# Conformer and DeltaNet trunk step: where the memory values stand in the convolution, which engine sums, and two margins of the planner

## The chip, the core and the metric

The kernel runs on one of the eight cores of one Trainium2 chip. A core has five engines that run side by side and wait for each other by semaphores: TensorE (PE in the profile; PEld is its weight load), VectorE (DVE), ScalarE (ACT), GpSimd (POOL) and SyncE (SP), which issues most DMAs. SBUF is the on-chip working memory, PSUM the memory of eight banks into which TensorE writes its sums. The metric is the device time of one execution in microseconds, and the figure for a kernel is the median of its runs.

## The reference

One inference step of a two-layer encoder runs for two groups of tokens that share all weights: 256 prompt tokens of one new stream and 16 tokens of each of eight running streams, 384 tokens of 1024 features. Each layer is a feed-forward half-step, a token mixer, a cross-attention into 256 memory tokens and a second feed-forward half-step, each with a norm before and after. The mixer is a Conformer convolution in layer 0 and a gated DeltaNet in layer 1. The change is in and around the convolution:

```python
u = h @ w_in + b_in
val, gate = jnp.split(u, 2, axis=-1)
u = val * jax.nn.sigmoid(gate)
hist = jnp.concatenate([conv_buf.astype(u.dtype), u], axis=1)
c = causal_depthwise_conv(hist, dw) + dw_b          # 31 taps on each feature
c = jax.nn.silu(layer_norm(c, ln_g, ln_b))
return c @ w_out + b_out, hist[:, -(CONV_W - 1):]
```

The memory keys and values of the prompt, `mem_prompt @ xa_wk` and `mem_prompt @ xa_wv` of both layers, are outputs too. They depend on no token, so they can be computed anywhere ahead of the attention that reads them.

## The kernel before

**Three matmuls for one.** Weights lie in device memory as chunks of 128 x 1024 fp32 numbers. `get` (L295) loads a chunk into one of three `raw` buffers, ScalarE casts it to the shorter type fp32r (`whi`), and the rest, the low part `wlo`, is the difference of the two. It is taken by VectorE, or by GpSimd where the chunk is listed in `SLOW` (L92). Eight pairs `whi`, `wlo` are held at a time, taken in the order of the calls. Activations are split in the same way (`hTh`, `hTl`, and `rbh`, `rbl`), and each product is three fp32r matmuls. Sums, transposes and the memory keys go through TensorE in fp32 instead, where one matmul leaves two records in the profile.

**Emission and planner.** The program is first emitted as a list of operations for each engine, by generators that stand for tasks beside each other (`spawn`, `pump`, `until`). They keep rough clocks of their own, and the buffers and PSUM banks are handed out in this emission. Then `Scheduler` (L323) builds the dependence graph of all operations and orders every engine's queue: a list schedule by priority (`early`), whose priorities come from a schedule run backwards (`late`), in three passes, of which the shortest plan is kept (`order`). `LAT` (L327) has the planner's delay from the end of an operation on one engine to the start of a dependent one on another. What depends on nothing urgent fills gaps. Each engine carries out its queue strictly in that order.

**The convolution** (`conv`, L1060). Features lie on partitions, 128 of them in each of eight tiles (`KT`), tokens on the free axis. For each tile, two projections (`cg`, `cv`) of 24 fp32r matmuls of 384 columns each give gate and value; `glu` forms the gated input and its history. The task `taps` takes the tiles in pairs: VectorE multiplies and adds one tap after the other into two PSUM banks (the taps that read only the cache of running streams were done during the first feed-forward). When a pair is finished, TensorE adds its two tiles into the mean, with a matrix of 1/1024 (`onesd`, L1125), and a PSUM bank is held for that sum from the first pair on.

**Memory values** (`kv_split`, L942) are emitted behind the eight tiles. They load the memory tokens into `rbh` and `rbl`, and for each layer and head one unit of two chunks and 48 fp32r matmuls of 256 columns, eight units in all, each with a PSUM bank, a copy and a store. **Memory keys** (`kv`, L1006) are units of eight fp32 matmuls of 256 columns; `KV` says how many are emitted at each place: three at the end of the first feed-forward, five behind the convolution's tiles, two with its output projection.

**The layer norm** (`ln`, L1155) goes by three groups of 128 tokens. VectorE subtracts the mean, ScalarE squares, TensorE sums the squares of the eight feature tiles with eight matmuls against `onesd` (L1171), VectorE adds EPS, GpSimd takes the power of -1/2, TensorE spreads the result over the partitions with a matmul against the identity, VectorE multiplies, and ScalarE applies the silu. Then the output projection (`co`) follows group by group, with a norm chain (`chain`, L663) behind each group that leads to the attention's first matmuls.

Of the kernel before, what the change touches and what calls it, by code (L numbers as in the profile page):

```python
# [11 lines left out]
ALU = mybir.AluOpType  # L12
# [3 lines left out]
P = 128  # L16
# [21 lines left out]
FIRST_SLOW = 2  # L38
# [12 lines left out]
POOLTRUE = 1  # L51
LANES = 8
# [270 lines left out]
class Scheduler:  # L323
# [3 lines left out]
    LAT = {"P": {"P": 0, "A": 197, "V": 197}, "A": {"P": 275, "V": 131, "G": 159, "A": 131},  # L327
           "V": {"P": 260, "A": 128, "V": 127, "G": 155}, "G": {"P": 311, "A": 77, "V": 76, "G": 104}}
# [113 lines left out]
    def early(self, prio):  # L442
# [12 lines left out]
        for _ in ops:  # L455
            best, e, i = self.pick(free, now, later, lambda i: -prio[i])
            o = ops[i]
            cost = o.cost
            if o.nbytes:
                best = max(best, lanes[e][0])  # L460
            at[i] = best
            if o.table and o.table != table:
                table = o.table
                cost += 1283.0
            end = free[e] = best + cost
            if o.nbytes:
                dma = max(dma, end + DMA_IN) + o.nbytes / 360.0
                end = dma + DMA_OUT
                lanes[e] = lanes[e][1:] + [end]
            last = max(last, end)  # L470
            for j in o.succ:
                rd[j] = max(rd[j], end + (0.0 if o.nbytes else self.LAT[e].get(ops[j].eng, 150)))
                npred[j] -= 1
                if not npred[j]:
                    heapq.heappush(later[ops[j].eng], (rd[j], j))
# [66 lines left out]
class Model:  # L542
# [399 lines left out]
    def kv_split(self):  # L942
# [3 lines left out]
        vt = E.vt  # L946
# [14 lines left out]
        for l in range(2):  # L961
            for h in range(XH):

# [16 lines left out]
                E.store(self.O["pkv"][l, h][:, 512:1024], r)  # L980
        self.free(rh)
        E.vt = vt
# [77 lines left out]
    def conv(self, chains, post, pre):  # L1060
# [32 lines left out]
        def taps():  # L1093
            for c0 in range(0, KT, 2):
# [26 lines left out]
                if not means:  # L1121
                    means.append((yield from self.gbank()))
                for c in cs:
                    self.free(hist[c][1], hist[c][3])
                    E.mm(means[0][0][:, 0:NTOK], self.onesd, cO[:, c, :], c == 0, c == KT - 1)  # L1125
            self.conv_end = e

        means = []
# [3 lines left out]
        for c in range(KT):  # L1132
# [9 lines left out]
            if c + 2 < KT:  # L1142
                prefetch(c + 2)

        self.kv_split()
# [9 lines left out]
        def ln(t, dep):  # L1155
# [11 lines left out]
            e = E.act(qv, x, AF.Square, dep=e)  # L1167
            yield e
            o, b = yield from self.gbank()
            for k in range(KT):  # L1170
                e = E.mm(o[:, 0:P], qv[:, k, :], self.onesd, k == 0, k == KT - 1)  # L1171
# [752 lines left out]
```

## Time and profile before

| | |
|---|---|
| median of 3 runs | 1880.22 us (1877.89 to 1883.22) |
| profiled execution, device time | 1880.99 us |
| its span, first to last instruction | 1879.2 us |
| TensorE busy (matmul) | 1848.6 us, 98% |
| VectorE busy | 986.4 us, 52% |
| ScalarE busy | 765.5 us, 41% |
| GpSimd busy | 252.6 us, 13% |
| granted TensorE clock, mean | 0.998 of full speed |

Busy time counts the time in which at least one instruction of the engine is under way. Matmuls overlap in the pipeline, so the duration of one record is longer than what it adds to the engine's time; the step from one start to the next shows that. The convolution begins with its first projection at 321.4 us, its taps end at 457.7 us, and its output projection begins at 474.6 us. A row of a timeline joins instructions of the same kind that follow each other; `x28` is their number.

### The profile page before, as it was taken

To read this page: it belongs to the slowest core of one execution; us is meant where nothing else is said; L and a number is where in the kernel's file an instruction comes from. 1 tells how busy PE (TensorE), PEld (TensorE's weight loads), DVE (VectorE), ACT (ScalarE), POOL (GpSimd) and SP (SyncE) were. 2 spreads that over 40 slices of the span, in tenths; PEclk is the share of its full clock that TensorE was granted. 3 is DMA by queue.
4 is the path that set the end of the run, shared out by engine and by line. 5 is a ranking of instruction groups with operands and counts; after the bars stand their busy time and mean duration, and the time that the engine had idled before them with its cause. 6 is when DMAs were issued, how large, how long until landed. Compare 5 with 4: busy or idle time off the path is not lost.

```text
span 1879.2 us, 26770 instructions
## 1 busy us (share of the span) xinstructions
PE 1848.6 (98%) x10479; PEld 1658.3 (88%) x10479; DVE 986.4 (52%) x1681; ACT 765.5 (41%) x1443; POOL 252.6 (13%) x420
## 2 busy tenths in 40 slices
PE   8999999999999999999999999999999999999998
PEld 7988998998877799999899999899998777899997
DVE  5456335898542643333643333687877644533333
ACT  4332334334542532323533333676665544432332
POOL 1000003568100100000200000233231101000000
PEclk9999999999999999999999999999999999999999
DMA  8534435448487534444434344333334583534441
GB/s 303 163 119 128 135 113 148 128 141 258 165 302 275 153 113 129 128 124 134 155 114 128 120 131 124 107 102 104 103 118 154 193 328 108 157 124 124 135 123 45
DMA packets 88622, 279.81 MB, mean 149 GB/s; under 512 B 17904, under 2 KB 20464, under 8 KB 88496
## 3 DMA queue, kind: packets, MB, share of 16 engines
q1 hardware_dynamic: 86368, 272.47, 45.4%
q0 software_dynamic: 2128, 5.63, 0.9%
q8 instruction: 82, 1.34, 0.3%
q14 instruction: 44, 0.36, 0.1%
HBM read 266.14 MB, written 11.92 MB: 148 GB/s over the span
## 4 chain that ended last, share of the span: by engine, by line
PE 63%; ACT 2%; DVE 2%; DMA 1%; POOL 1%; issue 1%; DVEq 0%; POOLq 0%; ACTq 0%; SPq 0%
PE ps L253 60%; PE ps L265 2%; PE ps L285 2%; DMA raw<-in_w 1%; DVE wlo L203 1%; ACT big L196 1%; POOL stat L203 1%; DVE big L216 1%; ACT whi L195 1%; PE ps L278 0%; ACT L196 0%; ACT hTl L196 0%; DVE hTl L203 0%; ACT big L195 0%; POOL stat L210 0%
## 5 line engine op out<-in xcount | busy, mean ns | idle before, releaser
L203 DVE TENSOR_TENSOR wlo<-raw,whi 128x1024 fp32r<-128x1024 f32 x341 | 415.3, 1223 | 566.9 <-ACT whi L195 564.8
L195 ACT CAST whi<-raw 128x1024 fp32r<-128x1024 f32 x377 | 393.7, 1050 | 710.7 <-PE ps L253 615.3
L253 PE MATMUL ps<-hTh,whi 128*128 128x384 f32 (+1 forms) x1680 | 505.6, 341 | 1.7 <-ACT big L196 0.7
L253 PE MATMUL ps<-hTl,whi 128*128 128x384 f32 (+1 forms) x1680 | 501.7, 339 | 0.1
L253 PE MATMUL ps<-hTh,wlo 128*128 128x384 f32 x1680 | 500.1, 339 | 0.0
L253 PEld LDWEIGHTS ps<-hTh,whi 128*128 128x128 f32 x1680 | 309.7, 188 | 14.4 <-ACT big L196 6.1
L253 PEld LDWEIGHTS ps<-hTl,whi 128*128 128x128 f32 x1680 | 310.2, 188 | 10.3 <-issue 2.8
L253 PEld LDWEIGHTS ps<-hTh,wlo 128*128 128x128 f32 x1680 | 309.6, 188 | 5.9 <-issue 0.7
L253 PE MATMUL ps<-whi,rbh 128*128 128x512 f32 (+1 forms) x800 | 242.2, 379 | 2.4 <-DVE big L216 2.3
L253 PE MATMUL ps<-whi,rbl 128*128 128x512 f32 (+1 forms) x800 | 244.1, 378 | 0.0
L253 PE MATMUL ps<-wlo,rbh 128*128 128x512 f32 (+1 forms) x800 | 240.9, 377 | 0.6 <-POOL wlo L203 0.6
L253 PE MATMUL ps<-big 128*128 128x128 f32 (+3 forms) x1144 | 216.0, 316 | 9.4 <-DMA big<-in_w 6.8
L253 PEld LDWEIGHTS ps<-big 128*128 128x128 f32 x1144 | 178.6, 192 | 36.8 <-issue 13.0
L253 PEld LDWEIGHTS ps<-wlo,rbh 128*128 128x128 f32 x800 | 150.2, 189 | 26.6 <-issue 1.6
L253 PEld LDWEIGHTS ps<-whi,rbh 128*128 128x128 f32 x800 | 149.2, 189 | 26.0 <-ACT big L196 2.6
L253 PEld LDWEIGHTS ps<-whi,rbl 128*128 128x128 f32 x800 | 150.1, 189 | 22.4 <-issue 0.8
L210 POOL TENSOR_SCALAR stat<-stat 128x1 f32<-128x1 f32 (+2 forms) x48 | 17.6, 367 | 1023.1 <-ACT hTl L196 1004.5
L203 DVE TENSOR_TENSOR big<-big,ps 128x384 f32<-128x384 f32 (+4 forms) x131 | 67.4, 521 | 81.5 <-PE ps L253 64.3
L216 DVE SCALAR_TENSOR_TENSOR ps<-big,cols,ps 128x384 f32<-128x384 f32 (+12 forms) x232 | 107.4, 553 | 0.4
L203 POOL TENSOR_TENSOR wlo<-raw,whi 128x1024 fp32r<-128x1024 f32 x36 | 86.7, 2421 | 49.5 <-ACT whi L195 43.7
L253 PE MATMUL ps<-whi,hTh 128*128 128x512 f32 x240 | 86.6, 402 | 2.5 <-ACT hTh L195 2.1
L253 PE MATMUL ps<-whi,hTl 128*128 128x512 f32 x240 | 85.4, 400 | 0.0
(91 smaller groups left out, 1488.8 us busy)
## 6 DMA issues: line engine op xcount, KB each, us to landing
raw<-in_w SPq DMA_DIRECT2D x380, 512.0 KB, 4.0
big<-in_ck SPq DMA_DIRECT2D x32, 512.0 KB, 6.0
big<-in_cv SPq DMA_DIRECT2D x32, 512.0 KB, 6.0
big<-in_w SPq DMA_DIRECT2D x21, 512.0 KB, 6.4
big<-in_npre SPq DMA_DIRECT2D x8, 512.0 KB, 7.4
big<-in_npost SPq DMA_DIRECT2D x8, 512.0 KB, 6.5
big<-out_pkv SPq DMA_DIRECT2D x8, 512.0 KB, 5.8
big<-in_state SPq DMA_DIRECT2D x8, 512.0 KB, 4.4
```

The costliest lines, as they stand in the source:

```text
L195: return self._on("A", cost, dep, lambda: sc.copy(out, in_), [in_], w)
L196: return self._on("A", cost, dep, lambda: sc.activation(out, in_, func, **kw), [in_, bias, scale] + ([] if after is None else [after]), w, ...
L203: return self._on(eng, cost, dep, lambda: e.tensor_tensor(out=out, in0=a, in1=b, op=op), [a, b], [out])
L210: return self._on(eng, cost, dep, lambda: e.tensor_scalar(out=out, in0=a, scalar1=s1, scalar2=s2, op0=op0, **kw), [a, s1, s2 if s2 is not ...
L216: lambda: v.scalar_tensor_tensor(out=out, in0=a, scalar=s, in1=b, op0=op0, op1=op1), [a, s, b], [out])
L253: self._add("P", cost, lambda: t.matmul(out, lhsT, rhs, start=start, stop=stop, **kw), [lhsT, rhs], [out])
L265: t.matmul(out, lhsT, rhs, start=start, stop=stop)
L285: self._add("P", 109.0, lambda: t.transpose(out, in_, ident), [in_, ident], [out])
```

## The change

- Low parts: `FIRST_SLOW` goes from 2 to 4, so VectorE instead of GpSimd takes the low parts of the four chunks of convolution tiles 2 and 3. Tiles 4 to 7, the values and the output projection stay with GpSimd.
- Memory values: `kv_split` becomes a generator with a pause ahead of each unit. `conv` advances it once behind each tile from tile 2 (`VFROM`) on: behind tile 2 the memory tokens are loaded, behind tiles 3 to 7 one unit each is emitted, and the last three follow behind the tiles.
- Mean: GpSimd adds tiles 0 to 5 into `total`. One matmul for `total` and one each for tiles 6 and 7 form the mean, in place of eight. The PSUM bank of the mean is taken at the third pair.
- Squares: VectorE sums the eight feature tiles of each group with one reduction from 128 x 1024 to 128 x 128 (`rsum`, L236), and one matmul follows in place of eight.
- Planner: in `LAT`, the delays from ScalarE, VectorE and GpSimd to TensorE are 150 ns longer, and `early` adds 107 ns (`RESTART`) to a TensorE operation that starts more than 10 ns after the operation before it ended.

```diff
--- before.py
+++ after.py
@@ -35,7 +35,8 @@
 OLD = 10
 CHB = 4000.0
 RUSH = 10000.0
-FIRST_SLOW = 2
+FIRST_SLOW = 4
+VFROM = 2
 ORD = 12000.0
 NRUSH = 3
 SLOTS = 3
@@ -49,6 +50,7 @@
 TAIL = 3
 PASSES = 3
 POOLTRUE = 1
+RESTART = 107.0
 LANES = 8
 DMA_IN, DMA_OUT = 650.0, 950.0
 HOP = 100.0
@@ -324,8 +326,8 @@
 
 
 
-    LAT = {"P": {"P": 0, "A": 197, "V": 197}, "A": {"P": 275, "V": 131, "G": 159, "A": 131},
-           "V": {"P": 260, "A": 128, "V": 127, "G": 155}, "G": {"P": 311, "A": 77, "V": 76, "G": 104}}
+    LAT = {"P": {"P": 0, "A": 197, "V": 197}, "A": {"P": 425, "V": 131, "G": 159, "A": 131},
+           "V": {"P": 410, "A": 128, "V": 127, "G": 155}, "G": {"P": 461, "A": 77, "V": 76, "G": 104}}
 
     def __init__(self, ops):
         self.ops = ops
@@ -462,6 +464,8 @@
             if o.table and o.table != table:
                 table = o.table
                 cost += 1283.0
+            if e == "P" and best > free[e] + 10.0:
+                cost += RESTART
             end = free[e] = best + cost
             if o.nbytes:
                 dma = max(dma, end + DMA_IN) + o.nbytes / 360.0
@@ -943,7 +947,6 @@
 
 
         E = self.E
-        vt = E.vt
         mh, ml = (a.rearrange("p k c -> p (k c)")[:, 0:2 * D] for a in (self.rbh, self.rbl))
         for i in range(2):
             c = slice(i * D, (i + 1) * D)
@@ -960,6 +963,8 @@
 
         for l in range(2):
             for h in range(XH):
+                yield
+                vt = E.vt
 
                 o, b = self.bank()
                 ws = [E.get(("v2", l, h, q)) for q in range(2)]
@@ -978,8 +983,8 @@
                 r = result(o, 512)
                 self.bfree(b)
                 E.store(self.O["pkv"][l, h][:, 512:1024], r)
+                E.vt = vt
         self.free(rh)
-        E.vt = vt
 
     def early(self, what, order):
 
@@ -1091,6 +1096,7 @@
             ready[c] = e
 
         def taps():
+            total, th = yield from self.galloc(NTOK)
             for c0 in range(0, KT, 2):
                 cs = (c0, c0 + 1)
                 while not all(c in ready for c in cs):
@@ -1118,13 +1124,23 @@
                             e = E.stt(o, h[:, :, j - TOLD:j - TOLD + BL], w, blk(a[:, 0:NTOK]), ALU.mult, ALU.add, dep=dep)
                     yield E.ck["V"] - 1200
                 self.bfree(ab)
-                if not means:
+                if c0 == KT - 4:
                     means.append((yield from self.gbank()))
                 for c in cs:
                     self.free(hist[c][1], hist[c][3])
-                    E.mm(means[0][0][:, 0:NTOK], self.onesd, cO[:, c, :], c == 0, c == KT - 1)
+
+                    if c == 1:
+                        E.tt(total, cO[:, 0, :], cO[:, 1, :], ALU.add, dep=e, eng="G")
+                    elif 1 < c < KT - 2:
+                        E.tt(total, total, cO[:, c, :], ALU.add, dep=e, eng="G")
+                    elif c >= KT - 2:
+                        E.mm(means[0][0][:, 0:NTOK], self.onesd, cO[:, c, :], False, c == KT - 1)
+                if c0 == KT - 4:
+                    E.mm(means[0][0][:, 0:NTOK], self.onesd, total, True, False)
+            self.free(th)
             self.conv_end = e
 
+        values = self.kv_split()
         means = []
         tapper = E.spawn(taps())
         prefetch(0)
@@ -1141,8 +1157,12 @@
             E.bonus = 0.0
             if c + 2 < KT:
                 prefetch(c + 2)
-
-        self.kv_split()
+            if c >= VFROM:
+
+                next(values, None)
+
+        for _ in values:
+            pass
         self.kv(KV["conv"])
         E.wait(tapper)
         mean, mb = means[0]
@@ -1165,10 +1185,13 @@
             qv = q.rearrange("p (k c) -> p k c", k=KT)
             yield e - 300
             e = E.act(qv, x, AF.Square, dep=e)
+            qs, qsh = yield from self.galloc(P)
+            yield e
+            e = E.rsum(qs, q.rearrange("p (k c) -> p c k", k=KT), dep=e)
             yield e
             o, b = yield from self.gbank()
-            for k in range(KT):
-                e = E.mm(o[:, 0:P], qv[:, k, :], self.onesd, k == 0, k == KT - 1)
+            e = E.mm(o[:, 0:P], qs, self.onesd, True, True)
+            self.free(qsh)
             v, r = self.st(1), self.st(1)
             e = E.ts(v, o[:, 0:1], EPS, ALU.add, dep=e)
             e = E.tt(r, v, self.negh[:, 0:1], ALU.pow, dep=e, eng="G")
```

## Rows read from the trace of the kernel before

**Rows 1.** The page, part 1: busy us, share, instructions by engine.
```profile
PE 1848.6 (98%) x10479; PEld 1658.3 (88%) x10479; DVE 986.4 (52%) x1681; ACT 765.5 (41%) x1443; POOL 252.6 (13%) x420
```

**Rows 2.** Stretches: length, busy us of each engine (instructions), clock, DMA, GB/s.
```profile
306.80:321.40 14.60, 11.71 (x62) 9.60 (x60) 11.13 (x14) 8.38 (x19) 9.32 (x15) 1.00 0.53 144
321.40:333.00 11.60, 11.60 (x66) 11.25 (x66) 1.72 (x4) 3.99 (x7) 1.95 (x2) 1.00 0.54 147
333.00:457.70 124.70, 120.08 (x771) 115.48 (x769) 120.85 (x266) 47.28 (x63) 85.23 (x57) 0.99 0.60 172
374.90:378.20 3.30, 3.30 (x15) 3.30 (x14) 3.30 (x9) 0.26 (x1) 0.00 (x0) 0.50 0.49 168
457.70:474.60 16.90, 16.90 (x106) 15.20 (x104) 8.77 (x11) 13.07 (x22) 11.55 (x11) 1.00 0.71 241
474.60:514.90 40.30, 40.23 (x187) 33.17 (x185) 19.68 (x24) 21.66 (x46) 4.65 (x13) 1.00 0.49 162
1190.00:1470.00 280.00, 278.99 (x1952) 258.37 (x1952) 211.32 (x532) 170.98 (x490) 77.62 (x205) 1.00 0.37 121
```

**Rows 3.** TensorE's timeline around one mean matmul: start us, us, instructions.
```profile
400.42 0.81 PE L253 MATMUL ps<-big 128*128 128x384 f32 x2
...
401.18 0.28 PE L253 MATMUL ps<-wlo,rbh 128*128 128x256 f32 x1
401.30 0.28 PE L253 MATMUL ps<-whi,rbl 128*128 128x256 f32 x1
```

**Rows 4.** TensorE's timeline, the matmuls of the squares.
```profile
461.29 5.95 PE L253 MATMUL ps<-big 128*128 128x256 f32 x50
467.07 0.39 PE L253 MATMUL ps<-ident,stat 128*128 128x128 f32 x2
```

**Rows 5.** Groups of TensorE, 474.6 to 514.9: busy us, mean ns, idle before.
```profile
L253 PE MATMUL ps<-big 128*128 128x256 f32 x26 | 7.6, 378 | 0.0
```

**Rows 6.** The same groups, 457.7 to 474.6.
```profile
L253 PE MATMUL ps<-big 128*128 128x256 f32 x32 | 8.2, 379 | 0.0
```

**Rows 7.** GpSimd's timeline ahead of the convolution.
```profile
304.89 2.48 POOL L203 TENSOR_TENSOR wlo<-raw,whi 128x1024 fp32r<-128x1024 f32 x1 [0.33 <-ACT whi L195]
...
316.40 2.34 POOL L203 TENSOR_TENSOR wlo<-raw,whi 128x1024 fp32r<-128x1024 f32 x1
318.71 0.56 POOL L203 TENSOR_TENSOR stat<-stat,negh 128x1 f32<-128x1 f32 x1
```

**Rows 8.** VectorE's timeline there; in brackets the idle time before and its releaser.
```profile
302.00 1.23 DVE L203 TENSOR_TENSOR wlo<-raw,whi 128x1024 fp32r<-128x1024 f32 x1 [1.20 <-ACT whi L195]
303.14 0.68 DVE L203 TENSOR_TENSOR big<-ps,big 128x512 f32<-128x512 f32 x1
...
305.06 3.53 DVE L216 SCALAR_TENSOR_TENSOR x<-big,stat,x 128x512 f32<-128x512 f32 x2
...
310.56 3.52 DVE L216 SCALAR_TENSOR_TENSOR big<-x,stat,big 128x512 f32<-128x512 f32 x2
314.00 1.40 DVE L216 SCALAR_TENSOR_TENSOR x<-big,stat,x 128x512 f32<-128x512 f32 x2
...
319.31 1.41 DVE L216 SCALAR_TENSOR_TENSOR big<-x,stat,big 128x512 f32<-128x512 f32 x2 [3.30 <-POOL stat L203]
```

**Rows 9.** VectorE's timeline, its two idle gaps among the taps.
```profile
370.80 1.22 DVE L203 TENSOR_TENSOR rbl<-raw,rbh 128x1024 fp32r<-128x1024 f32 x1 [1.66 <-ACT rbh L195]
...
402.04 0.74 DVE L216 SCALAR_TENSOR_TENSOR big<-ps,cols,big 128x256 f32<-128x256 f32 x2 [1.81 <-ACT big L196]
```

**Rows 10.** TensorE's timeline, its longest gap among the taps.
```profile
372.69 0.35 PE L253 MATMUL ps<-whi,rbh 128*128 128x256 f32 x1 [2.33 <-DVE big L216]
```

**Rows 11.** VectorE's timeline in the layer norm.
```profile
464.67 0.16 DVE L210 TENSOR_SCALAR stat<-ps 128x1 f32<-128x1 f32 x1 [2.35 <-PE ps L253]
...
467.57 1.22 DVE L203 TENSOR_TENSOR big<-big,ps 128x1024 f32<-128x1024 f32 x1
```

**Rows 12.** Groups of VectorE: the strided reduction.
```profile
L239 DVE TENSOR_REDUCE big<-big 128x96 f32<-128x384 f32 x8 | 6.8, 850 | 0.0
```

## The prediction

> **What bounds the kernel now.** I read the engine totals first, then the stages around the convolution, then one timeline per engine there. TensorE is busy 1848.6 of 1879.2 us [rows 1], so the whole kernel runs at the rate of its matmuls, and an edit far from TensorE pays only where TensorE stands idle. In the convolution this is less plain [rows 2]: from 333.0 us, where VectorE begins the taps, to 457.7 us, where it ends them, VectorE is busy 120.9 of 124.7 us and TensorE 120.1. Both are full at once, because the matmuls of the memory values and keys fill TensorE while VectorE works off the taps. Ahead of that, from the last down-projection (306.8) to the first convolution matmul (321.4), TensorE only does fillers and transposes and is idle 2.9 us. After it (457.7 to 474.6, the layer norm) VectorE is half idle and TensorE full again. So this stage has two limits, the bill of matmuls and VectorE's chain, and each edit is priced against both.
>
> **TensorE's bill.** A mean matmul (fp32, 384 columns, two records) began at 400.42, and the second fp32r matmul behind it at 401.18. Less one 256-column matmul (0.12, from 401.18 to 401.30), that is 0.64 us [rows 3]. Eight become three, which saves 5 x 0.64 = 3.2 us. The 24 matmuls of the squares and one key matmul run from 461.29 to 467.07 as 50 records [rows 4]. Less 2 x 0.215 for the key matmul (0.32 for a 384-column record, by columns), 5.35 us are left, 0.223 each. Twenty-four become three, which saves 21 x 0.223 = 4.7 us. The bill falls by 7.9 us. Nothing else is added to TensorE or taken from it; the 384 matmuls of the memory values are the same ones elsewhere.
>
> **Does the bill reach the end?** The stage up to the first output matmul is also held by VectorE, so a freed microsecond inside it shows only if TensorE does later work there. There is some: behind the layer norm, between 474.6 and 514.9, stand 26 records of 256 columns that belong to memory keys [rows 5], 26 x 0.215 = 5.6 us on a TensorE that is busy 40.2 of 40.3 us [rows 2]. They depend on nothing in the convolution and fill whatever hole comes first. With the squares gone from the layer norm they move there, and the stretch behind shortens by up to 5.6 us. Bounds 0 (none moves) and 5.6; I take 5.6, since the same kind of record already fills the layer norm (32 of them between 457.7 and 474.6, [rows 6]).
>
> **The low parts of tiles 2 and 3 leave GpSimd.** Three of the four GpSimd low parts fall into the norm before the convolution, the first at 304.89, the last at 316.40, 2.3 to 2.5 us each [rows 7]. VectorE's pair of scale-and-add instructions takes 1.40 us at 314.00, but 3.53 us at 305.06 and 3.52 us at 310.56, exactly where a GpSimd low part is under way [rows 7, 8]: 2.1 us lost twice. The third low part stands in GpSimd's queue between the sum and the power at 318.71, and VectorE waits 3.30 us for that power at 319.31 [rows 7, 8]: some 2.3 us. Together that is 6.5 us on the chain that ends in the first convolution matmul. Against it VectorE gets four low parts at 1.14 us from start to start (302.00 to 303.14, [rows 8]), 4.6 us, of which some can lie in its idle 9.9 us between 321.4 and 333.0 [rows 2]. TensorE has two key units and transposes to do in the meantime, which would reach to about 319.7 without its idle 2.9 us. Bounds: a gain of 6.5 (all relief, all low parts hidden) and a loss of 4.6 (no relief, none hidden). I take a gain of 2.0, what TensorE's fillers leave.
>
> The Trainium skill, page "SBUF — State Buffer", section "Who interferes with whom", has the rule behind the slow pairs: a VectorE instruction with two SBUF inputs and a GpSimd instruction that reads SBUF exclude each other for a whole instruction. By it the trace agrees, 3.53 against 1.40 us; and it speaks against the change too, since the four moved low parts have two SBUF inputs and would now be the ones shut out. That is the rival "swapped" below.
>
> **Memory values between the tiles.** In front of the values the chain has two holes on VectorE, 1.66 us at 370.80, waiting for the cast of the memory tokens, and 1.81 us at 402.04, waiting for the gate's sigmoid [rows 9]. TensorE meanwhile waits 2.33 us, until 372.69, for VectorE's last instruction of a tap pair, which frees a PSUM bank [rows 10]. With the memory tokens loaded at tile 2, one values unit after each later tile, and the mean's bank taken only at the third tap pair, both holes can go. Bounds: 0 and a gain of 3.5. I take 1.5, about one of two. The tap work itself, 266 instructions, stays. Interleaved, tiles 4 to 7 cost GpSimd four low parts per step, 4 x 2.4 = 9.6 us [rows 7], and about 1 us for an add (0.91 by proportion of 384 to 1024 columns; bounds 0.56, one of a single column, and 2.4 [rows 7]), against 14.4 us of TensorE per step (96 records: 48 of 384 columns by 0.18, 48 of 256 by 0.12). So GpSimd's queue keeps up with 2.5 us of stores beside, with little to spare. What waits behind it is the next low part, not the taps.
>
> **The layer norm.** Before, the first variance was taken up at 464.67, and the multiply began at 467.57 because the broadcast matmul stood behind the other tiles' squares on TensorE, until 467.07 [rows 4, 11]. Now three reductions of 1024 elements to 128 stand on VectorE. The trace has none. A plain instruction of 1024 elements takes 1.22 us; the strided reduction of 384 elements takes 0.85, or 2.27 by proportion [rows 11, 12]. Ours is strided too, so I take 2.0. The first variance then comes about 1.7 us later (it waits behind two reductions), the broadcast 1.4 us sooner, and the multiply queues behind the third reduction: 0.7 us later. Bounds: 1.3 earlier with 1.22, 2.4 later with 2.27 three times in a row.
>
> **The planner's margins** change only the order: 150 ns more before a matmul may follow another engine, 107 ns after each hole. TensorE's idle time outside 306.8 to 474.6 is 30.6 - 2.9 - 4.6 = 23.1 us with the start and the end of the kernel in it, and the delta stage, which is most dependent on chains, has 1.0 us in 280 [rows 1, 2]. All 23 can't go, since the first load and the last norm stay; a loss would come from chain steps that go behind a filler now (0.12 to 0.22 us each), so it takes some 40 such steps on the path to lose 7. Between these ends far apart I take 0, nearest to the delta stage's row, with 5 either way in the range.
>
> **Sum.** The start of the output matmuls moves by -2.0 - 1.5 + 0.7 = -2.8 us, the stretch behind it by -5.6: -8.4 us. By the bill alone it is -7.9, so idle time would hardly change; the two views agree. The profiled execution took 1880.99 us (span 1879.2 and 1.8 around it) and gives 1872.6. The median is 0.8 lower, 1880.22, so I predict 1871.8.
>
> TensorE's granted clock fell to 0.50, the 1.2 GHz level, at 374.9 after the hole of 2.33 us before 372.69, over a stretch of 3.3 us [rows 2, 10]; at half the rate that is a loss of 1.7 us. The Trainium skill, page "TensorE: Matmul & The Clock Gate", section "The HAM clock gate", says that idleness brings the lower clock. By that rule a stage with 7.9 us less matmul work could fall twice more: 1875.2. I leave it to the range.
>
> **Rivals.**
> *The hole stays.* The key units don't move forward, because their weights or banks come no sooner; VectorE sets the stage and TensorE just idles where squares and means were. For it: VectorE's 97% from 333.0. Against: 32 such records already ran in the layer norm. Only the 2.8 us come, or 1.1 with reductions at the bound: 1877.4 to 1879.1, about 1878. That the change does not do what it says belongs here too: the planner orders all instructions anew, and if it had values between the tiles already, the move in the code does nothing.
> *Swapped (slower).* VectorE becomes the sole bound: its four low parts land on the chain between 295 and 320, beside GpSimd low parts that now are those of the values, so the blocked pairs remain and nothing is relieved. The low parts cost 4.6, two of them blocked for 2.1 us each 4.2, and the reductions, on the same engine, 2.4: +11.2, less 5.6 for the fillers, so +5.6: 1886.6 for the profiled execution, 1885.8 as a median. It decides once a GpSimd low part still runs before 320. For it: VectorE is 76% busy there already. Against it: the loads are taken up in order, and the values' chunks come after those of tile 2.
> *All of it.* The relief is whole (6.5), both VectorE holes go (3.5), reductions are cheap (1.3) and the fillers move (5.6): -16.9, 1863.3. It needs TensorE without any hole from 306.8 to 474.6, where it now has 7.5 us of idle time and 1.7 of slow clock.
>
> **Chances.** Forecast 0.55 (its own range 1867.5 to 1875.5), hole stays 0.20, swapped 0.12, all of it 0.13. A measurement of this kernel can tell 0.3%, 5.6 us, from no change: faster is under 1874.6, slower over 1885.9. Faster: most of the forecast and all of the last rival, 0.64. Slower: half of swapped and a bad planner's order, 0.11. The same: 0.25. The range 1862 to 1881 leaves out swapped and the far end of the last rival.
>
> **What would show it.** No GpSimd low part between 300 and 320 and both VectorE pairs there at 1.4 us; the first convolution matmul near 319; tap work still ending 123 to 125 us after it began; 6 TensorE records of 384 columns for the mean instead of 16, and 6 for the squares instead of 48; a reduction row near 2.0 us; fewer key records behind the first output matmul. I am wrong if VectorE's tap stretch grows, if TensorE's idle time grows by more than 4 us, or if the stages from 534 us on change by more than 5 us.

## The result, and the profile after

The changed kernel takes 1868.18 us (median of 4 runs, 1865.76 to 1869.38) against 1879.39 for the kernel before (4 runs): ratio 0.9936, 95% interval 0.9917 to 0.9955. That is 11.2 us faster, where 8.4 were forecast. The profiled execution took 1869.38 us, with a span of 1867.6. Helper lines are two higher than before: L205 is the add and low part, L218 scale-and-add, L255 the matmul, L198 the activation, L241 the reduction.

The engine totals after, for [rows 1]:

```profile
PE 1839.2 (98%) x10427; PEld 1652.7 (88%) x10427; DVE 994.2 (53%) x1688; ACT 765.8 (41%) x1441; POOL 248.1 (13%) x421
```

TensorE has 52 instructions less, as the change says: 10 records of the mean and 42 of the squares. The stretches after, for [rows 2] (same columns): ahead of the convolution, its first projections, the taps, the layer norm, the output projection with the first attention matmuls, and a slow piece of the delta stage.

```profile
301.00:313.30 12.30, 12.23 (x65) 10.11 (x62) 11.73 (x17) 8.06 (x20) 5.22 (x10) 1.00 0.50 146
313.30:326.20 12.90, 12.90 (x77) 12.74 (x76) 5.57 (x8) 6.39 (x9) 2.36 (x6) 1.00 0.70 225
326.20:443.20 117.00, 115.37 (x762) 112.17 (x761) 116.65 (x261) 43.89 (x60) 85.16 (x61) 1.00 0.61 166
443.20:463.70 20.50, 17.68 (x82) 13.89 (x80) 13.58 (x15) 13.01 (x21) 14.42 (x11) 1.00 0.87 284
463.70:520.80 57.10, 55.72 (x266) 43.79 (x266) 33.66 (x39) 31.77 (x63) 11.34 (x19) 1.00 0.67 223
1199.40:1202.60 3.20, 3.20 (x17) 3.20 (x17) 3.19 (x13) 3.17 (x4) 0.51 (x2) 0.50 0.00 0
```

Where the time went shows only when both traces are cut at the same instructions. This table is worked out from the first or last instruction of each stage, in one profiled execution of each kernel, with the boundaries rounded to 0.1 us. A: start, to the first projection. B: first feed-forward, to its last down-projection. C: from there to the first convolution matmul. D: to the first tap that adds into PSUM. E: taps, to the end of the last one that does. F: layer norm, to the first output matmul. G: output projection, to its last matmul. H: delta stage, from its first projection to its first output matmul. I: from there to the first output matmul of the second attention. The two stretches left out, between G and H and behind I, differ from the kernel before by 2 us at most.

| us | A | B | C | D | E | F | G | C to G | H | I | span |
|---|---|---|---|---|---|---|---|---|---|---|---|
| before | 24.3 | 281.9 | 15.2 | 12.8 | 122.4 | 17.9 | 61.0 | 229.4 | 286.2 | 111.4 | 1879.2 |
| after | 24.0 | 277.0 | 12.3 | 12.9 | 117.0 | 20.5 | 57.1 | 219.8 | 289.6 | 114.0 | 1867.6 |
| e1 margins alone | 23.8 | 278.1 | 15.3 | 12.3 | 119.0 | 18.2 | 57.4 | 222.2 | 288.2 | 111.8 | 1868.5 |
| e2 no margins | 23.7 | 277.9 | 12.6 | 12.6 | 116.5 | 22.9 | 56.0 | 220.6 | 288.4 | 114.3 | 1870.0 |
| e3 low parts back | 24.8 | 280.8 | 12.4 | 11.9 | 116.7 | 19.6 | 57.2 | 217.7 | 288.2 | 113.9 | 1868.6 |
| e4 values behind, with the hole | 22.1 | 279.6 | 12.0 | 12.5 | 151.7 | 19.5 | 57.0 | 252.7 | 287.0 | 112.3 | 1897.0 |
| e5 values behind | 22.1 | 277.8 | 10.9 | 12.3 | 122.8 | 21.0 | 56.3 | 223.4 | 288.3 | 114.7 | 1870.8 |
| e6 squares back | 22.3 | 277.2 | 12.3 | 12.9 | 118.2 | 20.4 | 56.6 | 220.5 | 288.7 | 114.3 | 1866.2 |
| e7 mean back | 22.3 | 275.4 | 12.8 | 12.9 | 121.8 | 20.9 | 55.8 | 224.2 | 287.1 | 111.1 | 1863.0 |
| e9 both sums back | 22.3 | 275.4 | 12.3 | 12.9 | 121.0 | 26.0 | 55.3 | 227.5 | 288.3 | 111.8 | 1869.2 |
| e8 first squares on TensorE | 22.2 | 276.9 | 12.3 | 12.9 | 117.0 | 17.3 | 57.0 | 216.5 | 288.5 | 114.0 | 1863.3 |
| e10 before, +50 ns | 22.9 | 282.1 | 15.4 | 14.0 | 122.3 | 24.1 | 58.0 | 233.7 | 287.9 | 111.8 | 1885.2 |
| e11 e8 with 100 ns | 22.4 | 277.8 | 12.2 | 12.9 | 117.0 | 17.6 | 56.6 | 216.3 | 288.6 | 113.5 | 1865.4 |
| e12 e8 with 200 ns | 21.6 | 279.5 | 12.3 | 12.8 | 116.5 | 18.9 | 56.1 | 216.5 | 291.1 | 111.6 | 1864.3 |

The convolution gave 9.6 us of the span's 11.6, the first feed-forward another 4.9, and the delta stage and second attention took 6.0 back. Six key records (1.3 us) that stood in B before stand elsewhere after.

Part of such differences is TensorE's clock and not the order. The granted clock was 0.50, the 1.2 GHz level, in E of the kernel before (at 374.9, [rows 2]), and in H of the change (in the stretches above) and in its A:

```profile
11.50:14.80 3.30, 3.30 (x9) 2.67 (x8) 1.42 (x2) 1.40 (x6) 1.52 (x3) 0.50 1.02 394
```

In the traces of the experiments it fell in A (e2), D (e10), E (e2, e5, e7, e10), F (e9, e10) and H (e1, e2, e9, e11, e12), four times in e4, and nowhere between 17 and 1860 us in e3, e6 and e8. Such a stretch cost 1.6 us in H (last section).

VectorE's timeline ahead of the convolution after the change, for [rows 8] (start us, us, instructions, idle time before and its releaser):

```profile
299.86 1.40 DVE L218 SCALAR_TENSOR_TENSOR x<-big,stat,x 128x512 f32<-128x512 f32 x2
...
302.37 1.22 DVE L205 TENSOR_TENSOR wlo<-raw,whi 128x1024 fp32r<-128x1024 f32 x1
...
305.51 1.41 DVE L218 SCALAR_TENSOR_TENSOR x<-big,stat,x 128x512 f32<-128x512 f32 x2 [0.44 <-POOL stat L205]
...
308.70 1.21 DVE L205 TENSOR_TENSOR wlo<-raw,whi 128x1024 fp32r<-128x1024 f32 x1
...
310.43 1.41 DVE L218 SCALAR_TENSOR_TENSOR big<-x,stat,big 128x512 f32<-128x512 f32 x2
311.76 1.22 DVE L205 TENSOR_TENSOR rbl<-raw,rbh 128x1024 fp32r<-128x1024 f32 x1
...
314.88 1.23 DVE L205 TENSOR_TENSOR rbl<-raw,rbh 128x1024 fp32r<-128x1024 f32 x1 [1.30 <-ACT rbh L197]
```

All pairs take 1.4 us, the wait of 3.30 us for GpSimd is down to 0.44, and the two low parts of the memory tokens (`rbl`), which stood among the taps (one is in [rows 9]), now come before the first tap.

In the layer norm, groups (443.2 to 463.7 us, for [rows 6]; columns as in [rows 5]) and then VectorE's, GpSimd's and ScalarE's timelines, for [rows 11]:

```profile
L255 PE MATMUL ps<-big 128*128 128x256 f32 x55 | 13.3, 381 | 0.9 <-DMA big<-in_w 0.9
...
L255 PE MATMUL ps<-big 128*128 128x128 f32 x6 | 1.2, 274 | 0.0
```

```profile
446.22 3.48 DVE L205 TENSOR_TENSOR big<-big,ps 128x1024 f32<-128x1024 f32 x3 [2.33 <-PE ps L255]
450.28 3.85 DVE L241 TENSOR_REDUCE big<-big 128x128 f32<-128x1024 f32 x2 [0.58 <-ACT big L198]
454.05 0.15 DVE L212 TENSOR_SCALAR stat<-ps 128x1 f32<-128x1 f32 x1
454.11 1.93 DVE L241 TENSOR_REDUCE big<-big 128x128 f32<-128x1024 f32 x1
455.96 1.21 DVE L205 TENSOR_TENSOR big<-big,ps 128x1024 f32<-128x1024 f32 x1
```

```profile
454.82 4.68 POOL L205 TENSOR_TENSOR wlo<-raw,whi 128x1024 fp32r<-128x1024 f32 x2
459.47 1.06 POOL L205 TENSOR_TENSOR stat<-stat,negh 128x1 f32<-128x1 f32 x2
```

```profile
457.25 1.28 ACT L198 ACT_TABLE_LOAD   x1 [2.21 <-DVE stat L212]
...
461.64 1.04 ACT L197 CAST whi<-raw 128x1024 fp32r<-128x1024 f32 x1
462.58 1.03 ACT L197 CAST hTh<-big 128x1024 fp32r<-128x1024 f32 x1
```

The key records went from 32 to 55 in the layer norm, and none is left behind the first output matmul. The three reductions hold VectorE, and the second and third power wait on GpSimd behind two low parts.

One thing has no row ahead of the prediction: weight loads (PEld) in the first feed-forward waiting for ScalarE's silu. The waits of the kernel before, from 30 to 285 us (sum us, times, longest), and of the kernel after:

```profile
PEld ps L253 <- ACT big L196: 5.8, 11, 0.7
```

```profile
PEld ps L255 <- ACT big L198: 0.4, 1, 0.4
PEld ps L255 <- DVE big L205: 0.2, 1, 0.2
```

### The profile page after: what moved, and what is told of

It reads as the page before. It is cut to its first block, busy times and chain, and to the rows that moved or that the text cites. A ratio compares the mean times of both kernels' runs of the same rounds, so it can differ in the third digit from the quotient of the medians.

```text
span 1867.6 us, 26681 instructions
## 1 busy us (share of the span) xinstructions
PE 1839.2 (98%) x10427; PEld 1652.7 (88%) x10427; DVE 994.2 (53%) x1688; ACT 765.8 (41%) x1441; POOL 248.1 (13%) x421
## 5 line engine op out<-in xcount | busy, mean ns | idle before, releaser
L205 DVE TENSOR_TENSOR wlo<-raw,whi 128x1024 fp32r<-128x1024 f32 x345 | 419.0, 1222 | 549.8 <-ACT whi L197 496.9
L255 PE MATMUL ps<-hTh,whi 128*128 128x384 f32 x1680 | 510.9, 340 | 0.9 <-ACT big L197 0.6
L255 PE MATMUL ps<-hTl,whi 128*128 128x384 f32 (+1 forms) x1680 | 510.5, 339 | 0.7 <-DVE hTl L205 0.7
L255 PE MATMUL ps<-hTh,wlo 128*128 128x384 f32 x1680 | 503.3, 338 | 0.0
L255 PEld LDWEIGHTS ps<-hTh,whi 128*128 128x128 f32 x1680 | 310.3, 188 | 12.6 <-issue 2.8
L255 PEld LDWEIGHTS ps<-hTl,whi 128*128 128x128 f32 x1680 | 310.3, 188 | 8.7 <-DVE hTl L205 1.0
L255 PEld LDWEIGHTS ps<-hTh,wlo 128*128 128x128 f32 x1680 | 309.9, 188 | 4.9 <-issue 0.4
L255 PE MATMUL ps<-whi,rbh 128*128 128x512 f32 (+1 forms) x800 | 242.4, 379 | 1.1 <-DMA raw<-in_w 1.1
L255 PE MATMUL ps<-wlo,rbh 128*128 128x512 f32 (+1 forms) x800 | 239.9, 376 | 0.0
L255 PE MATMUL ps<-whi,rbl 128*128 128x512 f32 (+1 forms) x800 | 238.4, 376 | 0.0
L255 PE MATMUL ps<-big 128*128 128x128 f32 (+3 forms) x1092 | 205.0, 318 | 11.4 <-DMA big<-in_w 7.8
L255 PEld LDWEIGHTS ps<-big 128*128 128x128 f32 x1092 | 174.5, 194 | 37.7 <-issue 9.6
L255 PEld LDWEIGHTS ps<-whi,rbh 128*128 128x128 f32 x800 | 148.7, 188 | 24.2 <-issue 2.4
L255 PEld LDWEIGHTS ps<-wlo,rbh 128*128 128x128 f32 x800 | 149.2, 188 | 23.1 <-issue 0.4
L255 PEld LDWEIGHTS ps<-whi,rbl 128*128 128x128 f32 x800 | 149.2, 188 | 22.7
L205 DVE TENSOR_TENSOR big<-big,ps 128x384 f32<-128x384 f32 (+4 forms) x131 | 67.4, 520 | 109.4 <-PE ps L255 101.8
L218 DVE SCALAR_TENSOR_TENSOR ps<-big,cols,ps 128x384 f32<-128x384 f32 (+14 forms) x232 | 107.8, 555 | 0.4
L255 PE MATMUL ps<-whi,hTh 128*128 128x512 f32 x240 | 85.9, 400 | 1.2 <-ACT hTh L197 1.1
L255 PE MATMUL ps<-whi,hTl 128*128 128x512 f32 x240 | 85.2, 399 | 1.2 <-DVE hTl L205 1.0
L255 PE MATMUL ps<-wlo,hTh 128*128 128x512 f32 x240 | 83.4, 393 | 0.0
```

Source lines behind the costliest of these rows:

```text
L205: return self._on(eng, cost, dep, lambda: e.tensor_tensor(out=out, in0=a, in1=b, op=op), [a, b], [out])
L218: lambda: v.scalar_tensor_tensor(out=out, in0=a, scalar=s, in1=b, op0=op0, op1=op1), [a, s, b], [out])
L255: self._add("P", cost, lambda: t.matmul(out, lhsT, rhs, start=start, stop=stop, **kw), [lhsT, rhs], [out])
```

## The experiments

Ratios are against the kernel before; that of the change itself is 0.9936 (0.9917 to 0.9955).

**e1: the margins alone**, on the kernel before.

```diff
+RESTART = 107.0
-    LAT = {..., "A": {"P": 275, ...}, "V": {"P": 260, ...}, "G": {"P": 311, ...}}
+    LAT = {..., "A": {"P": 425, ...}, "V": {"P": 410, ...}, "G": {"P": 461, ...}}
+            if e == "P" and best > free[e] + 10.0:
+                cost += RESTART
```

> The kernel before with the planner's two margins alone (150 ns more into TensorE, 107 ns after a hole). Theory A (the margins take the small stalls out of the feed-forward steps): the first feed-forward's projections, 264 us before, take 5 to 7 us less, no stall of 0.28 us per step is left on TensorE, and the whole is 3 to 8 us faster, since the delta stage may lose some again. Rival B (the margins only reorder, as the prediction put it, and the first feed-forward gained by what was moved out of its end): within 2 us of before, and the first feed-forward unchanged.

Ratio 0.9964 (0.9952 to 0.9976), some 6.8 us, though no work changes. In the profile the feed-forward gives 3.8 us, and its silu wait falls to 2.4 us (helper lines are one higher here):

```profile
PEld ps L254 <- ACT big L197: 2.4, 7, 0.5
```

Stage C keeps its 15.3 us and its blocked pairs, here one pair of VectorE's and then the low part of GpSimd that lies over it:

```profile
300.83 3.51 DVE L217 SCALAR_TENSOR_TENSOR x<-big,stat,x 128x512 f32<-128x512 f32 x2
```

```profile
300.96 2.83 POOL L204 TENSOR_TENSOR wlo<-raw,whi 128x1024 fp32r<-128x1024 f32 x1
```

The convolution gives 7.1 us (C to G) without an edit in it: 3.4 in the taps and 3.6 in the output projection. Both holes of [rows 9] are gone from VectorE's timeline, though the values stand behind the tiles and both `rbl` parts among the taps:

```profile
351.33 1.22 DVE L204 TENSOR_TENSOR rbl<-raw,rbh 128x1024 fp32r<-128x1024 f32 x1
...
363.98 1.22 DVE L204 TENSOR_TENSOR rbl<-raw,rbh 128x1024 fp32r<-128x1024 f32 x1
```

**e2: the change without the margins.**

```diff
-    LAT = {..., "A": {"P": 425, ...}, "V": {"P": 410, ...}, "G": {"P": 461, ...}}
+    LAT = {..., "A": {"P": 275, ...}, "V": {"P": 260, ...}, "G": {"P": 311, ...}}
-            if e == "P" and best > free[e] + 10.0:
-                cost += RESTART
```

> The changed kernel with the old delays and no price for a hole in the planner. Theory A: it loses the 5 to 7 us of the first feed-forward and keeps the shorter tap stage (117 us from the first tap to the last), so 1872 to 1876 us. Rival B: no loss, 1867 to 1870 us, and the first feed-forward stays at about 257 us.

Ratio 0.9953 (0.9941 to 0.9965). The feed-forward is short here too (277.9, silu wait 0.3 us), so the margins are not what it needs: each half of the change alone takes that wait away. The halves are worth 6.8 and 8.8 us alone and 12.0 together. That suggests an overlap of 3.6 us, but the uncertainty of this difference is some 5 us.

**e3: low parts back on GpSimd.**

```diff
-FIRST_SLOW = 4
+FIRST_SLOW = 2
```

> The changed kernel with the low parts of convolution tiles 2 and 3 on GpSimd again. Theory A (a GpSimd low part shuts out VectorE's two-input instructions and delays the powers of the norm): pairs of scale-and-add near 3.5 us come back between 295 and 320 us, the stretch from the last down-projection to the first convolution projection grows from 12.4 to about 15 us, and the whole is 2 to 4 us slower than the changed kernel. Rival B (TensorE's fillers set that stretch): the blocked pairs come back but the whole stays within 1 us.

Ratio 0.9956 (0.9944 to 0.9968). The slow pairs and the long stage C did not come back: in this order GpSimd's low part lies between the pairs. GpSimd's and VectorE's timelines there:

```profile
305.78 2.37 POOL L205 TENSOR_TENSOR wlo<-raw,whi 128x1024 fp32r<-128x1024 f32 x1 [1.20 <-ACT whi L197]
```

```profile
304.47 1.41 DVE L218 SCALAR_TENSOR_TENSOR x<-big,stat,x 128x512 f32<-128x512 f32 x2
...
310.78 1.40 DVE L218 SCALAR_TENSOR_TENSOR x<-big,stat,x 128x512 f32<-128x512 f32 x2
```

The feed-forward is longer in this profile instead (280.8). So blocked pairs come from where the order puts the low parts, and another order is a way out as well as moving them to VectorE.

**e4: all values behind the tiles.**

```diff
-VFROM = 2
+VFROM = 8
```

> The changed kernel with all memory values emitted behind the eight tiles, as before. Theory A (the place of the values decides the two holes among the taps): the tap stretch goes from 117 back to 120 to 122 us, VectorE shows holes of 1.5 us or more in it again, and the whole is 3 to 6 us slower than the changed kernel. Rival B (the planner reorders them anyway, the holes went because the mean's bank was freed): the tap stretch stays at 117 to 118 us and the whole within 1.5 us.

Ratio 1.0116 (1.0103 to 1.0129): slower than before. VectorE's taps stop for 19.19 us (its timeline, idle time in brackets):

```profile
416.37 0.55 DVE L212 TENSOR_SCALAR ps<-big,cols 128x256 f32<-128x256 f32 x1 [19.19 <-ACT ps L197]
```

The kernel before has the same place without such a hole. The new form restores the emission clock `vt` behind each unit, where the old one did it once, behind all. All eight units then count as emitted at one instant, and by the code the task `taps` gets its PSUM banks for the third pair behind theirs.

**e5: the same with a running clock.**

```diff
-VFROM = 2
+VFROM = 8
                 yield
-                vt = E.vt
+                if (l, h) == (0, 0):
+                    vt = E.vt
-                E.vt = vt
+        E.vt = vt
```

> As the run before it with all values behind the tiles, but the emission's clock runs on through the eight units and is set back once at their end, as in the kernel before; in the run before it was set back after each unit. Theory A (the 19 us without taps came from the clock: the third tap pair asked for its PSUM banks only after all units had been given theirs): no VectorE hole over 3 us among the taps, a tap stretch of 117 to 122 us instead of 152, 1868 to 1873 us. Rival B (the place alone did it): the hole stays, 1895 us or more.

Ratio 0.9956 (0.9944 to 0.9968): the hole is gone, so the emission clock made it (that the banks are the link between them is read from the code only). The values' place as such is worth 3.6 us in C to G (223.4 against 219.8), and the taps take 5.8 more: the two `rbl` parts lie among them again, 4.7 us in place of none. The holes of [rows 9] don't come back.

**e6 and e7: squares and mean back on TensorE**, one at a time. With the mean, its PSUM bank is held from the first pair of tiles again.

```diff
 # e6
-            e = E.rsum(qs, q.rearrange("p (k c) -> p c k", k=KT), dep=e)
...
-            e = E.mm(o[:, 0:P], qs, self.onesd, True, True)
+            for k in range(KT):
+                e = E.mm(o[:, 0:P], qv[:, k, :], self.onesd, k == 0, k == KT - 1)
 # e7
-                if c0 == KT - 4:
+                if not means:
...
+                    E.mm(means[0][0][:, 0:NTOK], self.onesd, cO[:, c, :], c == 0, c == KT - 1)
```

> The changed kernel with the squares summed by TensorE's eight matmuls per group again. Theory A (the layer norm is a chain through VectorE, in which the reduction costs 1.93 us where the eight matmuls took 1.8, and TensorE has holes there anyway): the layer norm, 20.5 us from the last tap to the first output matmul, comes back to 17.5 to 19, the 4.7 us of matmuls fill holes or push key units behind, and the whole is within 2 us of the changed kernel. Rival B (TensorE's bill decides, as in the prediction): 4 to 5 us slower than the changed kernel.

> The changed kernel with the mean formed by eight matmuls again, the bank taken at the first pair. Theory A (TensorE's bill): 3.2 us more of matmuls and, with one bank less among the taps, 2 to 5 us slower than the changed kernel. Rival B (VectorE bounds the taps): within 1.5 us, the tap stretch still 117 us.

Ratios 0.9938 (0.9925 to 0.995) and 0.9937 (0.9923 to 0.995): no difference from the change that can be told. With the mean back the taps take 4.8 us more, and other stages (A, B, H, I) took 8.7 us less in that profile. An estimated 3 of these are the clock, at 1.6 us for each stretch at half rate: it fell in A and H of the change and in neither in e7.

**e9: both sums back.**

```diff
 # the edits of e6 and e7 together
```

> The changed kernel with both the mean and the squares on TensorE again, so that all 7.9 us of matmuls return; values, low parts and margins stay as changed. Each alone returned within 1 us of the changed kernel. Theory A (VectorE's chain bounds the stage, and the matmuls fall into holes): within 2 us of the changed kernel, 1865 to 1870 us. Rival B (the two stand in for each other: one saving is enough to free TensorE, and with both gone its bill decides): 4 to 8 us slower, 1871 to 1875 us.

Ratio 0.9943 (0.9931 to 0.9955), 1.3 us behind the change. With both intervals the difference is -2.9 to 5.5 us, so the 7.9 us of the bill are excluded. In the convolution of this profile as much is lost (C to G 227.5, 7.7 more), but most of it not by the bill: 5.5 stand in the layer norm, where ScalarE's first square waits until 452.81 for the landing of a store of memory keys or values, TensorE waits 2.75 us for that square, and its clock is at half rate from 453.2 to 460.1. The first row is a stretch, the second TensorE's timeline, the third ScalarE's:

```profile
453.20:460.00 6.80, 6.09 (x22) 5.59 (x23) 0.16 (x1) 5.20 (x8) 2.51 (x3) 0.50 0.36 129
```

```profile
453.91 4.63 PE L255 MATMUL ps<-big 128*128 128x128 f32 x18 [2.75 <-ACT big L198]
```

```profile
452.81 1.06 ACT L198 ACTIVATE big<-big 128x1024 f32<-128x1024 f32 x1 [7.70 <-DMA out_pkv<-big]
```

**e8: the first group's squares on TensorE**, the other two by reduction.

```diff
-            e = E.rsum(qs, q.rearrange("p (k c) -> p c k", k=KT), dep=e)
+            if t == 0:
...
+                for k in range(KT):
+                    e = E.mm(o[:, 0:P], qv[:, k, :], self.onesd, k == 0, k == KT - 1)
+            else:
...
+                e = E.rsum(qs, q.rearrange("p (k c) -> p c k", k=KT), dep=e)
```

> The changed kernel with the squares of the first group alone on TensorE, the other two on VectorE. Theory A (the first output matmul waits for the first group's chain, in which the reduction stands behind the three subtractions): the layer norm is 1 to 2 us shorter and the whole 0 to 2 us faster than the changed kernel, for 1.6 us more of matmuls. Rival B (the bill): 1.6 us slower.

Ratio 0.9941 (0.9926 to 0.9956). The layer norm does shrink, from 20.5 to 17.3 us: the first variance, at 449.15, no longer waits for two reductions. VectorE's timeline:

```profile
443.43 3.48 DVE L205 TENSOR_TENSOR big<-big,ps 128x1024 f32<-128x1024 f32 x3 [1.47 <-PE ps L255]
447.26 1.98 DVE L241 TENSOR_REDUCE big<-big 128x128 f32<-128x1024 f32 x1 [0.34 <-ACT big L198]
449.15 0.15 DVE L212 TENSOR_SCALAR stat<-ps 128x1 f32<-128x1 f32 x1
```

The profiled span is 4.3 us shorter, of which an estimated 3 are the clock's two falls in the change, which e8's profile does not have. The timed runs are not shorter by anything that can be told: the gain of a stage is below what the ratio can tell.

**e10: the kernel before with 50 ns more**, and **e11, e12: e8 with margins of 100 and 200 ns** in place of 150.

```diff
 # e10, on the kernel before
-    LAT = {..., "A": {"P": 275, ...}, "V": {"P": 260, ...}, "G": {"P": 311, ...}}
+    LAT = {..., "A": {"P": 325, ...}, "V": {"P": 310, ...}, "G": {"P": 361, ...}}
 # e11, on e8
+    LAT = {..., "A": {"P": 375, ...}, "V": {"P": 360, ...}, "G": {"P": 411, ...}}
 # e12, on e8
+    LAT = {..., "A": {"P": 475, ...}, "V": {"P": 460, ...}, "G": {"P": 511, ...}}
```

> The kernel before with 50 ns more in the planner's three delays into TensorE, a third of the margin, and nothing else. Theory A (the stalls of the first feed-forward, 5.8 us of weight loads that wait for the silu, are an accident of one order, which any other plan may lose): the first feed-forward falls from 282 to 276 to 279 us as with the full margin, the whole is 3 to 7 us faster. Rival B (the size of the margin does it): at least 3 us of those stalls stay and the whole is within 2 us of before.

> First group's squares on TensorE, with a margin of 100 ns in place of 150. Theory A (stages that no edit touches move by chance of the order): the convolution's layer norm stays at 17 to 18 us, while the delta stage and the second attention each move by up to 3 us either way; the whole 1860 to 1870 us. Rival B (150 ns is a fitted size): slower by 3 us or more than with 150.

> First group's squares on TensorE, with a margin of 200 ns in place of 150. Theory A: as with 100 ns, remote stages move by up to 3 us either way, the whole 1860 to 1870 us, with no trend in the margin. Rival B (the margin keeps gaining with its size, or has its best value at 150): a difference of 3 us or more with the sign that the run with 100 ns does not have, or slower on both sides.

Ratios 1.0021 (1.001 to 1.0032), 0.9947 (0.993 to 0.9963) and 0.9922 (0.991 to 0.9935). With e8 between them (0.9941) the time falls with the margin on that kernel, by 0.0025 from e11 to e12, with an uncertainty of 0.0021. On the kernel before it goes the other way: 50 ns make it slower, by 4 us, which neither expectation had, and leave its silu waits:

```profile
PEld ps L253 <- ACT big L196: 4.4, 9, 0.5
```

In its profile the loss stands in the layer norm (24.1 us). ScalarE's timeline has weight casts ahead of the squares, which begin at 465.46 (460.09 in the kernel before), and the granted clock is at half rate in D and F too:

```profile
465.46 2.94 ACT L196 ACTIVATE big<-big 128x1024 f32<-128x1024 f32 x3
```

```profile
320.20:323.60 3.40, 3.40 (x13) 3.17 (x11) 1.90 (x4) 1.21 (x4) 0.22 (x1) 0.50 1.11 342
466.90:470.30 3.40, 3.40 (x19) 3.40 (x18) 0.00 (x0) 2.79 (x3) 2.12 (x3) 0.51 0.97 302
```

So a longer margin is not by itself the better one. But e10 leaves out the price of a hole (`RESTART`), and no run has the 150 ns or the 107 ns alone. e12 has the lowest median of all, 1865.28 us, but its interval overlaps the change's.

## Why the prediction was right, and where its working was wrong

The direction, the range and nearly the size held, the size partly by luck. The four stages of the sum (C, E, F, G) gave 9.6 us where it had 8.4, with each of its terms off, and two changes that it did not have, 4.9 us gained in the feed-forward and 6.0 lost in H and I, nearly cancel.

**TensorE's bill: the count right, its worth wrong.** All 52 instructions went, but e6, e7 and e9 show that the kernel hardly profits: 1.3 us (-2.9 to 5.5) for 7.9. The sentence that failed is "by the bill alone it is -7.9 ... the two views agree". In the profiles the stages that no edit touches differ by as much as the saving: in e9 they are 6.1 us shorter, against 7.7 lost in the convolution. Of the 6.1, 1.7 are in A, where the clock fell in the change and not in e9 (24.0 and 22.3 us), and 2.2 in I, where TensorE waits 1.4 us for a transfer and 1.7 for ScalarE in the change and for neither in e9. Whether the order or that one execution made these waits is not shown. "The hole stays" fell with the moved fillers, and "all of it" had the convolution at -16.9, where it gave 9.6.

**Fillers: the size near, the cause wrong.** All records of [rows 5] moved forward and stage G gave 3.9 us, of 5.6. Two of the 26 began ahead of the first output matmul already; the 24 behind it are 5.2 us. The rest is refilled: 16 records of the attention (128x256 into 32 rows, 1.3 us of TensorE) now stand in their place, and with no key left TensorE waits for chain steps, 1.1 us for `hTh` just ahead of the stage and 1.0 for `hTl` in it. But the squares' leaving was not what moved them: e9 has both sums on TensorE and no key behind either. Nor does undoing the low parts (e3) or the values' place (e5) bring one back, while e1 and e10, without the edits of the convolution, keep 16 (by their starts). Even so their G is 3.5 and 3.0 us shorter than before. Which of these edits moves the records stays open.

**Low parts: right in place.** -2.9 us for -2.0, the pairs at 1.4 us, no GpSimd low part between 300 and 322. The first convolution matmul came at 313.3, not 319, since the feed-forward ended sooner. The prediction's 319.7 for the end of TensorE's fillers does not follow from its rows: 321.4 less 2.9 of idle time is 318.5. "Swapped" fell: the values' first low part of GpSimd comes behind this stage. e3 limits it: the relief can be had without the move. The Trainium skill, page "SBUF — State Buffer", section "Who interferes with whom", says that such pairs exclude each other for a whole instruction: e1's pair agrees, 3.51 us beside a GpSimd low part and 1.40 without.

**Values between the tiles: undersized, and not the cause by themselves.** The taps gave 5.4 us for 1.5. Both holes of [rows 9] went (3.5), the upper bound, and two `rbl` parts left the taps for the time ahead of them (2 x 1.14 = 2.3), which the prediction didn't price. Only the second part is shown to hang on the values' place (e5). The holes are gone in e1 and in e5 as well, with all values behind the tiles. And e7 and e9, with the values between the tiles but the mean back, take 121.8 and 121.0 us for the taps, so the 117.0 needs the mean's edit too. VectorE is now busy 116.65 of 117.0 us: this stage is at its bound.

**The layer norm: the operation right, its surroundings missed.** The reduction took 1.956 us (2.0 estimated), the first variance came 2.0 us later behind the subtractions (4.35 against 2.35), the multiply 1.0 sooner behind that (1.9 against 2.9). Not priced were 1.2 us ahead of the first subtraction, with key records between the mean's matmuls, and 0.7 behind the multiply, where a table load (1.28) and a weight cast (1.04) stand ahead of the first group's `hTh`. These four add to 2.9; the last tap into SBUF ends 0.4 sooner behind the last one into PSUM, so stage F took 2.5 more (17.96 to 20.43). The bound of 2.4 does not follow from the rows: three reductions of 2.27 behind the subtractions, which ended at 462.32 (464.67 less 2.35, [rows 11]), end at 469.13, 1.6 later than the old multiply began.

**The planner's margins: the step that failed most.** "0 with 5 either way" was argued from TensorE's idle time. The largest loss there was in no idle column: weight loads waiting 5.8 us for the silu while the page calls TensorE 98% busy, so the feed-forward's 4.9 us were not seen. The margins alone give 6.8, but e2 has the short feed-forward without them, so they are not the only way to that order. Whether in e1 it is the 150 ns, the price of a hole or just another order stays open. TensorE's clock, which the prediction left to the range, did not fall in the convolution of the change: it is 1.00 in all five stretches there.

Single undoings from the change cost 3.2 us (margins), 3.8 (low parts), 3.8 (values' place), 0.4 (squares) and 0.2 (mean), each with an uncertainty of some 4 us: the total is shown, its split is not. Whether a given order of the remote stages is better for a reason that could be foretold is open.

## What to carry to other kernels

In a kernel that a list scheduler orders, any edit redraws every stage: over these plans the first feed-forward took 275 to 282 us, the delta stage 286 to 291 and the second attention 111 to 115 with nearly the same work and the falls of TensorE's clock in it, so an edit worth less than some 4 us can't be told from that. A stage-by-stage table is needed beside the total, and before a stage's loss is laid to an edit, its waits have to be read: in e9 it was a store and the clock. Freed matmul time on a "98% busy" TensorE was no sure gain here, 1.3 us for 7.9; look at the waits of its weight loads too. Where a generator resets an emission clock, its buffers are handed out by that clock: 19 us hung on that line.

## What the runs showed of the hardware

The granted clock fell to 0.50, the 1.2 GHz level, in stage H of the change (1199.40 to 1202.60, in the stretches above), after TensorE had stood idle 0.47 us. The same sequence of records, with the same 0.47 us, ran without a fall in e3. All 14 traces have this idle time ahead of the same matmuls, 0.47 to 0.65 us; the clock fell behind it in six (the change, e1, e2, e9, e11, e12) and not in the other eight, the kernel before (0.48) among them. TensorE's timelines of the change and of e3:

```profile
1196.63 0.83 PE L255 MATMUL ps<-big 128*128 128x8 f32 x6 [0.47 <-DVE big L218]
...
1198.24 4.49 PE L255 MATMUL ps<-big 128*128 128x128 f32 x24
```

```profile
1199.10 0.83 PE L255 MATMUL ps<-big 128*128 128x8 f32 x6 [0.47 <-DVE big L218]
...
1200.71 2.90 PE L255 MATMUL ps<-big 128*128 128x128 f32 x24
```

That is 1.6 us of the 3.4 that stage H lost, by the clock and not by the order; whether it comes back in each execution isn't known, nor what decides it.

The strided reduction of 1024 fp32 elements took 1.956 us where the plain add of 1024 takes 1.2, and GpSimd's add of 384 columns 1.05, where 0.91 was estimated (groups of the change):

```profile
L241 DVE TENSOR_REDUCE big<-big 128x128 f32<-128x1024 f32 x3 | 5.8, 1956 | 0.6 <-ACT big L198 0.6
```

```profile
L205 POOL TENSOR_TENSOR big<-big 128x384 f32<-128x384 f32 x5 | 5.3, 1051 | 4.7 <-DVE big L218 4.6
```
